# Layer 2 of a two-layer trunk: the transposes of a head's probabilities moved one weight block later

## The chip, the cores and the metric

One core of one Trainium2 chip runs the whole kernel. The metric is the device time of one execution in microseconds (us). Before the change it is 1230.51 us, the median of 3 runs (1229.99 to 1230.73).

## The reference

The input is a sequence of 256 tokens of width 2048. Layer 1 is a Mamba-2 layer, layer 2 a sparse latent attention layer with 32 heads of 128. The part that the change touches is the attention of layer 2, once the queries, the latent keys and values and the selection of keys are there:

```python
logits = jnp.einsum('bthc,btkc->bthk', ql, kv_sel).astype(jnp.float32) * attn_scale
valid = sel <= tpos[None, :, None]
logits = jnp.where(valid[:, :, None, :], logits, -jnp.inf)
pr = jax.nn.softmax(logits, -1).astype(kv_sel.dtype)
return jnp.einsum('bthk,btkc->bthc', pr, kv_sel)
...
o = jnp.einsum('bthc,hcv->bthv', o_lat, w_uv).reshape(b, L, DSA_WIDTH)
return (o * jax.nn.silu(gate)) @ w_out
```

The kernel computes it per head with keys and values expanded, and with a mask (`mb`) in place of the gathered rows. All matrix products of weights are in float32, split into a high and a low part.

## The kernel before

**Stream of weight blocks.** All weights go through one stream of units (class `Stream`, lines 62 to 167). A unit is one block of 128 x 1024 weights. For each unit SyncE loads `raw` (L94), ScalarE rounds it to `hi` (L110), VectorE computes `lo = raw - hi` (L139), and TensorE then multiplies with both. There are 4 buffers each of `raw`, `hi` and `lo`. `run` works through the units by position: at position i it first writes out the conversions up to unit i + 3, then the matmuls of unit i, then one step of every generator that is active (older ones first), and a generator that starts at i is added last. Every engine takes its instructions in just this order, and nothing reorders them later. When `lo` of a unit is written, the load of the unit 4 further on is issued.

**Heads stage.** Units are laid out per pair of heads p: one block for keys and values (`pair_a`, called A here), one for queries (`pair_b`, B), then one or two gate blocks of two units each (ga, gb: first and second half of a gate, `stream_w`). So the layout repeats every 10 blocks: A B ga gb A B ga gb ga gb. Counted from the first A of the stage as block 0, block 40 is the A of pair 8. Each A and each B has 24 matmuls; each half of a gate has 8 matmuls of 512 columns (L328) and 8 of 256 columns (L325).

**A head's steps** (`head_steps`). One step is taken behind each block. Counted from the step of the logits:

- step 0: logits `lg` on TensorE (L937 to L940)
- step 1: mask, scale and row minimum on VectorE, from PSUM into the tile `lgs` (L948)
- step 2: exponentials on ScalarE (L953), in place
- step 3: reciprocal and scaling on VectorE (L956, L958), in place
- step 5: three transposes of `lgs` on TensorE into the PSUM tile `pt` (L964)
- step 6: copies of `pt` on ScalarE (L968, L969) and the low part on VectorE (L970)
- step 8: output `o` (po) on TensorE (L974 to L977)
- step 9 to 11: product with the gate on VectorE (L980), then rounding (L987, L989)

Heads 4k to 4k+3 start (step 0) in blocks 10k+4, 10k+6, 10k+8 and 10k+10. For the group of heads 12 to 15 (blocks 34 to 40) and what follows, the steps that use TensorE or the tile `lgs` fall like this in the kernel before:

| block | kind | TensorE behind the block, in order | L948 into `lgs` |
|---|---|---|---|
| 39 | gb | transposes of head 12 | head 14, then in the buffer of head 12 |
| 40 | A | logits of 15 | |
| 41 | B | transposes of 13 | head 15, then in the buffer of head 13 |
| 42 | ga | output of 12 | |
| 43 | gb | transposes of 14 | |
| 44 | A | output of 13, logits of 16 | |
| 45 | B | transposes of 15 | head 16, then in the buffer of head 14 |
| 46 | ga | output of 14, logits of 17 | |
| 47 | gb | | head 17, then in the buffer of head 15 |
| 48 | ga | output of 15, logits of 18 | |
| 49 | gb | transposes of 16 | head 18, then in the buffer of head 16 |

**Buffers.** `lgs` has 2 buffers, so head h + 2 takes the one of head h and may write it only when the transposes of head h have read it. Logits and outputs share 2 PSUM buffers (`y_tile`) in the order in which they are issued: the logits of 16 take the buffer that the output of 12 had (free when L980 of head 12 has read it, block 43), the output of 14 takes that of the output of 13 (L980 of head 13, block 45), the logits of 18 take that of the logits of 17 (L948 of head 17, block 47). `pt` has 2 buffers. Gate, key and value sums share 3 buffers (`acc_tile`).

**Evacuation** of keys, values and queries (`evac_steps`): high part on ScalarE (L926), low part on VectorE (L927), a plain copy on ScalarE (L928), and for values L915, L916, L917. The two engines wait for each other in it. Of a gate, ScalarE copies one half of the sum (L333), VectorE adds the other (L336), ScalarE takes a tanh (L726), VectorE multiplies (L728).

Of the kernel before, what the change touches and what calls it, by code (L numbers as in the profile page):

```python
# [171 lines left out]
def trunk_kernel(ctx: ExitStack, tc: tile.TileContext, x, xt, w1, wdt, dtp, prm, wo1,  # L172
# [20 lines left out]
    def y_tile(name):  # L193
        return p_y.tile([P, 512], F32, tag="y", name=name)

    def m_tile(name):
        return p_m.tile([P, 512], F32, tag="m", name=name)
# [734 lines left out]
    def head_steps(h):  # L932
        p, k = divmod(h, 2)
        (qh, ql, q1), (kh, kl, k1) = ([a[:, k, :] for a in PR[p][nm]] for nm in "qk")
        vh, vl, v2 = (a[:, k * P:(k + 1) * P] for a in PR[p]["v"])
        pl = y_tile(f"lg{h}")
        nc.tensor.matmul(pl[:, 0:128], q1, k1, start=True, stop=True)  # L937
        nc.tensor.matmul(pl[:, 128:384], qh, kh, start=True, stop=False)
        nc.tensor.matmul(pl[:, 128:384], qh, kl, start=False, stop=False)
        nc.tensor.matmul(pl[:, 128:384], ql, kh, start=False, stop=True)  # L940
        yield
        lg = d2.tile([P, 384], F32, tag="lg", name=f"lgs{h}")
        mx = d2.tile([P, 2], F32, tag="mx", name=f"mx{h}")
        sm = d2.tile([P, 2], F32, tag="sm", name=f"sm{h}")
        rn = d2.tile([P, 2], F32, tag="rn", name=f"rn{h}")
        parts = ((0, 0, 128), (1, 128, 384))
        for j, a, b in parts:
            v.tensor_tensor_reduce(out=lg[:, a:b], in0=pl[:, a:b], in1=mb[:, a:b],  # L948
                                   scale=-ATT_SCALE, scalar=3.0e38, op0=ALU.add, op1=ALU.min,
                                   accum_out=mx[:, j:j + 1])  # L950
        yield
        for j, a, b in parts:
            nc.scalar.activation(lg[:, a:b], lg[:, a:b], AF.Exp, scale=-1.0,  # L953
                                 bias=mx[:, j:j + 1], accum_out=sm[:, j:j + 1])
        yield
        v.reciprocal(rn, sm)  # L956
        for j, a, b in parts:
            v.tensor_scalar(lg[:, a:b], lg[:, a:b], rn[:, j:j + 1], 0.5,  # L958
                            op0=ALU.mult, op1=ALU.mult)
        yield  # L960
        yield
        pt = m_tile(f"pt{h}")
        for a in (0, 128, 256):
            nc.tensor.transpose(pt[:, a:a + 128], lg[:, a:a + 128], ident)  # L964
        yield
        ph, pl = (d2.tile([P, T], F32R, tag=f"prT{j}", name=f"prT{h}_{j}") for j in range(2))
        p2 = d2.tile([P, P], F32, tag="prT2", name=f"prT{h}_2")
        nc.scalar.activation(ph, pt[:, 0:T], AF.Copy)  # L968
        nc.scalar.activation(p2, pt[:, T:384], AF.Copy)  # L969
        v.tensor_sub(pl, pt[:, 0:T], ph.bitcast(F32))  # L970
        yield
        yield
        po = y_tile(f"o{h}")
        nc.tensor.matmul(po[:, 0:T], vh, ph, start=True, stop=False)  # L974
        nc.tensor.matmul(po[:, 0:T], vh, pl, start=False, stop=False)
        nc.tensor.matmul(po[:, 0:T], vl, ph, start=False, stop=False)
        nc.tensor.matmul(po[:, P:T], v2, p2, start=False, stop=True)  # L977
        yield
        og = d2.tile([P, T], F32, tag="og", name=f"og{h}", bufs=3)
        v.tensor_mul(og, po[:, 0:T], GT.pop(h))  # L980
        if h == 0:
            OG.append(big.tile([P, KT, 2 * T], F32R, tag="A", name="og0"))
        if h == 16:
            OG.append(big.tile([P, KT, 2 * T], F32R, tag="C", name="og1"))
        dst = OG[h // 16][:, h % 16, :]
        yield
        nc.scalar.activation(dst[:, 0:T], og, AF.Copy)  # L987
        yield
        v.tensor_sub(dst[:, T:2 * T], og, dst[:, 0:T].bitcast(F32))  # L989
        yield  # L990
# [3 lines left out]
    for p in range(NH2 // 2):  # L994
        src = wab[2 * p]
        i = st.add(wab[2 * p], 1024, pair_a(p), MOVING)
        st.side(i, (evac_steps, p, ("k", "v")))
        i = st.add(wab[2 * p + 1], 1024, pair_b(p), MOVING)
        st.side(i, (evac_steps, p, ("q",)))
        st.side(i + 3, (head_steps, 2 * p))  # L1000
        st.side(i + 5, (head_steps, 2 * p + 1))
        n = (left * (p + 1)) // 16 - (left * p) // 16
        for _ in range(n):
            add_gate(next(gates))
# [342 lines left out]
```

## Time and profile before

| | |
|---|---|
| median of 3 runs | 1230.51 us |
| the profiled execution, its own time | 1230.21 us |
| span of the profiled execution, first to last instruction | 1228.5 us |
| heads stage (block 0 to the first block of the output projection) | about 770 to 1039.6 us of the span |
| 10 blocks of the heads stage | 33.7 us |

The span is 1.7 us shorter than the execution's own time; what lies around it is not in the trace. The page of the profile gives busy times by engine, the chain of work that ended last, and groups of instructions; the trace behind it gives single instructions with their start, their duration, the idle time of the engine before them and what ended it. Matmuls are pipelined: one starts before the one before it has ended, so the distance of starts is what a matmul costs TensorE, and not its duration.

### The profile page before, as it was taken

The numbers are of one execution on the slowest core, as the hardware profiler recorded it, in microseconds if no ns is written. First come the engines' busy times: TensorE is split into PE (matmuls) and PEld (weight loads), VectorE is DVE, ScalarE is ACT, GpSimd is POOL, SyncE is SP. The second block draws the span as 40 slices with busy tenths as digits, with TensorE's granted clock in tenths as the row PEclk, the third lists the DMA queues.
The fourth block names the chain that finished last, engine by engine and source line by source line (L and its number), as shares of the span: only waits on it lengthen the run. The fifth ranks groups of instructions, "written<-read, shape, count | busy, mean of one in ns | idle before, by whom it ended". The sixth has DMA issues, their size and how long they took to land.

```text
span 1228.5 us, 19506 instructions
## 1 busy us (share of the span) xinstructions
PE 1222.3 (99%) x7195; PEld 1063.6 (87%) x7195; DVE 935.7 (76%) x1757; ACT 701.6 (57%) x1274; POOL 65.6 (5%) x102
## 2 busy tenths in 40 slices
PE   9999999999999999999999999999999999999998
PEld 7888888888888888788888898999999999888886
DVE  6978788988898889757557778877777777667457
ACT  5666566666666666544336655566766666433341
POOL 0001011001100110110000000000000000000000
PEclk9999999999999999999999999999999999999999
DMA  8765666566666665677666564554444445875552
GB/s 290 215 201 179 207 185 213 171 209 188 203 183 207 187 205 182 190 226 229 200 192 200 196 209 146 168 170 164 161 154 149 161 155 188 311 232 184 200 194 98
DMA packets 65790, 236.55 MB, mean 193 GB/s; under 512 B 8072, under 2 KB 8208, under 8 KB 65312
## 3 DMA queue, kind: packets, MB, share of 16 engines
q1 hardware_dynamic: 60784, 215.29, 54.4%
q0 software_dynamic: 4912, 20.02, 5.2%
q8 instruction: 57, 0.93, 0.3%
q14 instruction: 37, 0.30, 0.1%
HBM read 231.00 MB, written 4.28 MB: 192 GB/s over the span
## 4 chain that ended last, share of the span: by engine, by line
PE 97%; DVE 2%; DMA 1%; issue 0%; ACT 0%; SPq 0%; DVEq 0%
PE acc L328 24%; PE acc L325 12%; PE g L328 10%; PE o L556 9%; PE o L557 9%; PE o L558 9%; PE g L325 5%; PE y L453 2%; PE q L902 1%; PE q L901 1%; PE q L903 1%; PE pt L964 1%; DVE lo L139 1%; PE pxs L433 1%; PE k L879 1%; PE k L880 1%
## 5 line engine op out<-in xcount | busy, mean ns | idle before, releaser
L139 DVE TENSOR_TENSOR lo<-raw,hi 128x1024 fp32r<-128x1024 f32 (+1 forms) x404 | 488.8, 1213 | 236.6 <-ACT hi L110 236.1
L110 ACT ACTIVATE hi<-raw 128x1024 fp32r<-128x1024 f32 (+2 forms) x405 | 421.6, 1048 | 207.6 <-PE o L558 156.1
L328 PE MATMUL acc<-xT,hi 128*128 128x512 f32 x1280 | 314.6, 394 | 0.9 <-ACT hi L110 0.9
L328 PEld LDWEIGHTS acc<-xT,hi 128*128 128x128 f32 x1280 | 232.8, 188 | 46.7 <-ACT hi L110 1.3
L325 PEld LDWEIGHTS acc<-xT,lo 128*128 128x128 f32 x1280 | 159.3, 188 | 6.5 <-DVE lo L139 0.2
L325 PE MATMUL acc<-xT,lo 128*128 128x256 f32 x1280 | 162.0, 278 | 0.0
L328 PE MATMUL g<-x1T,hi 128*128 128x512 f32 x512 | 127.4, 395 | 0.0
L328 PEld LDWEIGHTS g<-x1T,hi 128*128 128x128 f32 x512 | 92.5, 188 | 17.5
L556 PE MATMUL o<-hi,yg 128*128 128x512 f32 x256 | 100.4, 392 | 0.0
L558 PE MATMUL o<-hi,yg 128*128 128x512 f32 x256 | 99.7, 390 | 0.0
L557 PE MATMUL o<-lo,yg 128*128 128x512 f32 x256 | 99.7, 389 | 0.0
L556 PE MATMUL o<-hi,og 128*128 128x512 f32 (+1 forms) x256 | 99.6, 389 | 0.0
L558 PE MATMUL o<-hi,og 128*128 128x512 f32 (+1 forms) x256 | 98.9, 386 | 0.0
L557 PE MATMUL o<-lo,og 128*128 128x512 f32 (+1 forms) x256 | 98.9, 386 | 0.0
L355 DVE SCALAR_TENSOR_TENSOR ca<-cr,par,ca 128x255 f32<-128x255 f32 x144 | 69.2, 480 | 3.4
L325 PE MATMUL g<-x1T,lo 128*128 128x256 f32 x512 | 69.4, 280 | 0.0
L325 PEld LDWEIGHTS g<-x1T,lo 128*128 128x128 f32 x512 | 65.8, 188 | 2.9
L358 ACT ACTIVATE cr<-ca 128x256 f32<-128x256 f32 x48 | 20.1, 418 | 79.0 <-DVE ca L355 79.0
L556 PEld LDWEIGHTS o<-hi,yg 128*128 128x128 f32 x256 | 48.1, 188 | 10.2 <-issue 0.2
L558 PEld LDWEIGHTS o<-hi,yg 128*128 128x128 f32 x256 | 48.1, 188 | 10.1
L558 PEld LDWEIGHTS o<-hi,og 128*128 128x128 f32 x256 | 48.1, 188 | 9.9
L557 PEld LDWEIGHTS o<-lo,yg 128*128 128x128 f32 x256 | 48.1, 188 | 9.7
(274 smaller groups left out, 1781.0 us busy)
## 6 DMA issues: line engine op xcount, KB each, us to landing
raw<-in_w_dram SPq DMA_DIRECT2D x159, 512.0 KB, 4.2
raw<-in_wo_dram SPq DMA_DIRECT2D x128, 512.0 KB, 3.6
raw<-in_wg_dram SPq DMA_DIRECT2D x64, 512.0 KB, 3.2
raw<-in_wab_dram SPq DMA_DIRECT2D x32, 512.0 KB, 3.2
abc<-acs_d POOLq DMA_DIRECT2D x32, 256.0 KB, 4.1
raw<-in_wcq_dram SPq DMA_DIRECT2D x8, 512.0 KB, 4.3
raw<-in_wkv_dram SPq DMA_DIRECT2D x8, 336.0 KB, 3.0
rx<-in_x_dram POOLq DMA_DIRECT2D x2, 1024.0 KB, 11.2
```

The costliest lines, as they stand in the source:

```text
L110: self.nc.scalar.activation(h[:, cs], r[:, cs], AF.Copy)
L139: eng.tensor_sub(*self.halfway.pop(i))
L325: nc.tensor.matmul(ps[:, 0:T], lw, xs[:, kt, 0:T], start=False, stop=last, skip_group_check=True)
L328: nc.tensor.matmul(ps, h[:, w], xs[:, kt, :], start=(kt == 0), stop=last, skip_group_check=True)
L355: v.scalar_tensor_tensor(acc[:, d:], rw[:, :T - d], w(k), acc[:, d:], op0=ALU.mult, op1=ALU.add)
L358: nc.scalar.activation(rw, acc, AF.Tanh)
L433: nc.tensor.transpose(pm[:, o:o + P], G[g][("x", 2 * half + c)][:, s * P:(s + 1) * P], ident)
L453: nc.tensor.matmul(py[ks, c * T + s * P:(c + 1) * T], xsT[:, s, c, ks], ms[c][k][:, ws], start=(c == 0 and s == 0), stop=(s == 1), skip_gr ...
L556: nc.tensor.matmul(ps, ah, hs, start=(kk == 2 * first), stop=False)
L557: nc.tensor.matmul(ps, ah, ls, start=False, stop=False)
L558: nc.tensor.matmul(ps, al, hs, start=False, stop=(kk == 31))
L879: nc.tensor.matmul(ps, h[:, o:o + P], ckvT[:, ct, 0:T], start=(ct == 0), stop=False)
```

## The change

The transposes of a head's probabilities (L964) move from step 5 to step 6. They are now issued directly ahead of the copies of the same head, behind the matmuls of the block and behind whatever older heads issue there. In the table above, those of head 12 move from block 39 to block 40, ahead of the logits of 15; of 13 from 41 to 42, behind the output of 12; of 14 from 43 to 44 and of 15 from 45 to 46, between an output and logits. L948 of head h + 2 stays where it is. The copies, the outputs and all later steps of a head stay where they are. No tile, buffer count or instruction is added or removed.

```diff
                             op0=ALU.mult, op1=ALU.mult)
         yield
         yield
+        yield
+
         pt = m_tile(f"pt{h}")
         for a in (0, 128, 256):
             nc.tensor.transpose(pt[:, a:a + 128], lg[:, a:a + 128], ident)
-        yield
         ph, pl = (d2.tile([P, T], F32R, tag=f"prT{j}", name=f"prT{h}_{j}") for j in range(2))
```

## Rows read from the trace of the kernel before

**Rows 1.** The profile's page: busy time by engine, the TensorE clock in 40 slices (9 is 90% or more), and the chain that ended last by engine.
```profile
PE 1222.3 (99%) x7195; PEld 1063.6 (87%) x7195; DVE 935.7 (76%) x1757; ACT 701.6 (57%) x1274; POOL 65.6 (5%) x102
...
PEclk9999999999999999999999999999999999999999
...
PE 97%; DVE 2%; DMA 1%; issue 0%; ACT 0%; SPq 0%; DVEq 0%
```

**Rows 2.** Busy time of each engine in stretches of 10 blocks (blocks 40 to 49 and 50 to 59): the length in us, then PE, PEld, DVE, ACT and POOL busy with their instructions, the granted clock as a share of full speed, the DMA share and GB/s.
```profile
904.54:938.25 33.71, 33.71 (x247) 31.59 (x246) 25.58 (x62) 22.65 (x57) 0.00 (x0) 1.00 0.46 158
938.25:972.15 33.90, 33.90 (x247) 31.70 (x246) 25.22 (x61) 22.53 (x57) 0.00 (x0) 1.00 0.45 153
```

**Rows 3.** The instructions that use the tile `lgs`: what their engine waited for, in us in total and how often.
```profile
  PE pt L964: 4.2, 8
```

**Rows 4.** VectorE in order of time, blocks 39 to 42: start, duration, operation, and in brackets the idle time before it and what ended it. L948 is that of head 14.
```profile
904.82 0.29 DVE L948 CUSTOM_DVE_ANT_0 lgs<-lg,mb 128x128 f32<-128x128 f32 x1 [0.54 <-PE pt L964]
...
905.86 1.22 DVE L139 TENSOR_TENSOR lo<-raw,hi 128x1024 fp32r<-128x1024 f32 x1 [0.39 <-ACT hi L110]
...
907.67 0.41 DVE L336 TENSOR_TENSOR gate<-g,gate 128x256 f32<-128x256 f32 x1
908.00 0.68 DVE L927 TENSOR_TENSOR hk<-k,hk 128x512 fp32r<-128x512 f32 x1
...
910.63 1.22 DVE L139 TENSOR_TENSOR lo<-raw,hi 128x1024 fp32r<-128x1024 f32 x1 [0.52 <-ACT hi L110]
...
913.31 0.42 DVE L927 TENSOR_TENSOR hq<-q,hq 128x256 fp32r<-128x256 f32 x1
915.13 1.23 DVE L139 TENSOR_TENSOR lo<-raw,hi 128x1024 fp32r<-128x1024 f32 x1 [1.40 <-ACT hi L110]
```

**Rows 5.** ScalarE in order of time, in the same stretch.
```profile
908.72 0.38 ACT L928 ACTIVATE hk<-k 128x256 f32<-128x256 f32 x1 [0.79 <-DVE hk L927]
...
909.52 1.07 ACT L110 ACTIVATE hi<-raw 128x1024 fp32r<-128x1024 f32 x1
...
913.77 0.39 ACT L928 ACTIVATE hq<-q 128x256 f32<-128x256 f32 x1 [2.39 <-DVE hq L927]
914.05 1.05 ACT L110 ACTIVATE hi<-raw 128x1024 fp32r<-128x1024 f32 x1
```

**Rows 6.** TensorE in order of time: the transposes of head 12, the logits of head 15, the first matmul of block 41 (a B) and the transposes of head 13 behind its 24 matmuls.
```profile
904.29 0.49 PE L964 MATMUL pt<-ident,lgs 128*128 128x128 f32 x3
...
907.41 0.38 PE L937 MATMUL lg<-hk,hq 128*128 128x128 f32 x2
...
907.99 0.28 PE L901 MATMUL q<-cqT,hi 128*128 128x256 f32 x1
...
910.79 0.49 PE L964 MATMUL pt<-ident,lgs 128*128 128x128 f32 x3
```

**Rows 7.** VectorE: the products with the gate of heads 12 and 13, the low part of unit 50 (block 47) and the last instruction of head 17's L948 in blocks 43 to 47.
```profile
918.53 0.42 DVE L980 TENSOR_TENSOR og<-o,sC 128x256 f32<-128x256 f32 x1
...
925.42 0.42 DVE L980 TENSOR_TENSOR og<-o,sC 128x256 f32<-128x256 f32 x1
...
930.68 1.22 DVE L139 TENSOR_TENSOR lo<-raw,hi 128x1024 fp32r<-128x1024 f32 x1 [0.67 <-ACT hi L110]
...
933.70 0.08 DVE L948 DVE_READ_ACCUMULATOR2_ANT mx<- 128x1 f32 x1
```

**Rows 8.** TensorE's weight loads that come first in the logits of 16 (block 44), the output of 14 (block 46) and the logits of 18 (block 48).
```profile
920.84 0.30 PEld L937 LDWEIGHTS lg<-hk,hq 128*128 128x128 f32 x2
...
927.36 0.19 PEld L974 LDWEIGHTS o<-prT,hv 128*128 128x128 f32 x1
...
934.57 0.30 PEld L937 LDWEIGHTS lg<-hk,hq 128*128 128x128 f32 x2
```

**Rows 9.** The same place 10 blocks later (block 57 and 58): the last weight load of the output of 19, the last instruction of head 21's L948 on VectorE and the first weight load of the logits of 22.
```profile
968.06 0.31 PEld L977 LDWEIGHTS o<-prT,hv 128*128 128x128 f32 x2
...
968.30 0.08 DVE L948 DVE_READ_ACCUMULATOR2_ANT mx<- 128x1 f32 x1
...
968.44 0.30 PEld L937 LDWEIGHTS lg<-hk,hq 128*128 128x128 f32 x2
```

**Rows 10.** The same place in the first group (blocks 17 and 18): head 5's L948 and the logits of 6.
```profile
832.26 0.08 DVE L948 DVE_READ_ACCUMULATOR2_ANT mx<- 128x1 f32 x1
...
833.43 0.30 PEld L937 LDWEIGHTS lg<-hk,hq 128*128 128x128 f32 x2
```

**Rows 11.** The chain that ended last in order of time: start and length of its pieces, with the number of instructions. Three transposes, the 8 matmuls of 512 columns behind them, 16 such matmuls behind matmuls of the stream, and the two matmuls that open the logits (L937: 128 columns in plain float32, as the transposes are; the stream's and most others are in the rounded type).
```profile
910.95 0.33 PE pt L964 x3
911.28 1.85 PE g L328 x8
...
929.69 3.65 PE g L328 x16
...
934.84 0.22 PE lg L937 x2
```

**Rows 12.** VectorE early in the output projection (units 87 and 88).
```profile
1055.40 1.23 DVE L139 TENSOR_TENSOR lo<-raw,hi 128x1024 fp32r<-128x1024 f32 x1 [3.00 <-ACT hi L110]
...
1059.73 1.22 DVE L139 TENSOR_TENSOR lo<-raw,hi 128x1024 fp32r<-128x1024 f32 x1 [2.78 <-ACT hi L110]
```

**Rows 13.** The page's DMA issues: loads of gate weights, count, size and median us to landing.
```profile
raw<-in_wg_dram SPq DMA_DIRECT2D x64, 512.0 KB, 3.2
```

## The prediction

> **What bounds the kernel now.** I read the page first: TensorE is busy 99% of the span, the chain that ended last runs 97% over it, and its granted clock is full in all slices [rows 1]. Then I read the heads stage in stretches of 10 blocks: TensorE is busy for every microsecond of 33.71, VectorE for 25.58 and ScalarE for 22.65 [rows 2]. So a change in this stage is worth what it does to TensorE: instructions that it spares, or waits that it puts in front of it. VectorE's and ScalarE's own idle time costs nothing until it reaches a buffer that TensorE wants. Then I asked who waits for the transposes: VectorE, in L948, for 4.2 us in 8 places, and nobody else of weight [rows 3]. That is one wait in each group of four heads, and it is the wait that this change moves.
>
> **Part 1, the transposes for themselves.** A turning is three transposes, 0.33 us on the chain; the 8 wide matmuls behind it take 1.85 us, where 16 such matmuls behind others take 3.65, or 1.83 for 8 [rows 11]. So a turning between two stretches of the stream costs 0.33 + 0.02 = 0.35 us. Between an output, which ends in plain float32, and logits, which begin so, I take three times what one of the two L937 takes, 3 x 0.11 = 0.33 [rows 11], with no second change of type. Saved: 0.02 us for each of 32 heads, 0.6 us in all. Not seen in the trace: transposes directly behind an output. Its bounds are no saving at all and the whole 0.35 us (32 x 0.35 = 11 us), but the three transposes are still issued and 0.33 of the 0.35 are theirs, so I take 0.02.
>
> **Part 2, the copies.** ScalarE's copies now follow their transposes in the same step, and wait for the end of the block. For head 12 that is some 1.6 us later than before; behind them in ScalarE's queue are the exponentials of head 14, which wait for L948 anyway (part 3). For heads 13 to 15 the copies come into ScalarE's queue after the transposes, once the delay of part 3 is counted. The output stands two blocks behind the copies as before. I cost this part at nothing; its cover is those two blocks, and without it the output would wait.
>
> **Part 3, L948 waits for a whole block.** L948 of head h + 2 needs the buffer of head h. For the first two heads of each group of four, heads h and h + 2 start 4 blocks apart, so L948 stands in step 5 of head h: until now directly behind the transposes, and after the change one block *ahead* of them. VectorE works in order, so it stands still until TensorE is through the next block and the transposes behind it. Nothing deadlocks: block 40 needs nothing that stands behind L948 of head 14.
>
> How much later: the transposes of head 12 start at 904.29, and L948 of head 14 at 904.82, 0.53 later [rows 4, 6]. After the change block 40 starts where those transposes did, and its 24 matmuls take 2.80 us (a block B with as many: 907.99 to 910.79 [rows 6]). So L948 starts 2.80 us later, at about 907.62. Queued behind it are the low part of unit 43, the low part of head 12's copies, the gate sum (L336), then keys and values of pair 8.
>
> What of it comes back: the low part of unit 43 had waited 0.39 us for ScalarE [rows 4]; ScalarE has it ready by then, so the lag falls to 2.80 - 0.39 = 2.41 us. From there on nothing comes back, and this is the point of the whole argument. The idle times of VectorE behind it (0.52 and 1.40 us in rows 4, 0.67 in rows 7) all end by ScalarE's rounding, and ScalarE's idle times ahead of those roundings (0.79 and 2.39 us [rows 5]) all end by VectorE's L927. The two hand work to and fro in evacuation: L927 at 913.31, L928 at 913.77, rounding at 914.05, low part at 915.13 [rows 4, 5]. So both keep a lag of 2.41 us, idle or not, up to L948 of head 17. The second L948 in this position (head 15, which now waits for head 13's transposes, behind block 42) adds none: by the same lag the L927 directly behind it (913.31 [rows 4]) comes at 915.7, and those transposes are read from about 914.7 on (907.09 + 0.33 + the logits' 0.58 + 2.80 for block 41 + 2.8 for block 42 + an output's 0.58 is 914.2, and 0.53 more).
>
> When TensorE meets it: it wants shared PSUM buffers. Handing over costs 0.06 us: where L948 of head 21 ended at 968.38, the weights of the logits were loaded at 968.44 and not, as usual, 0.2 us earlier [rows 9]. Margins before, less 0.06:
> - gate sum of block 39, wanted by block 42 at about 910.7: L336 ends 908.08 [rows 4] + 2.41 = 910.5. No wait, by 0.2 us.
> - logits of 16: L980 ends 918.95, the load starts 920.84 [rows 7, 8]: 1.83. Wait 0.58.
> - output of 14: 925.84 to 927.36: 1.46 [rows 7, 8]. TensorE is 0.95 late here.
> - logits of 18: L948 of head 17 ends 933.78, the load starts 934.57: 0.73 [rows 7, 8]. TensorE is 2.41 - 0.73 = 1.68 us late here.
>
> These don't add up, since the lag is carried by VectorE and ScalarE and each wait pays a part of it: the last and largest counts, 1.68 us for a group. Behind it comes the next L948 that waits for transposes, now behind block 50, and VectorE is there before TensorE: the lag begins anew and isn't summed.
>
> By groups: of 8, the last has its L948 in the output projection, where there are no evacuations and VectorE idles 3.00 and 2.78 us at a time [rows 12]; its cover is that idleness, and I cost it at nothing (if it went, at most another 1.7 us). Of the other seven, the first had a margin of 833.43 - 832.34 - 0.06 = 1.03 [rows 10], so 1.38 us; in the fifth the margin is already gone (blocks 50 to 59 take 33.90 us [rows 2, 9]), so 2.41; five take 1.68. Sum: 1.38 + 5 x 1.68 + 2.41 = 12.2 us. Since TensorE waits for VectorE in these groups, the savings of part 1 in them are not additional; only the last group's count, 0.1 us.
>
> **SyncE's loads** are issued when a low part is done, so some come 2.4 us later. A load lands in 3.2 us [rows 13] and its unit is rounded four units further on, over 10 us later; nothing waits. POOL has no work in these stretches [rows 2].
>
> **Sum.** 1230.21 + 12.2 - 0.1 = 1242.3 us against the profiled execution's own time; that one is 0.30 under the median of the runs, so 1242.6 for a median. I say 1242.5, +1.0%.
>
> **The rivals.**
> - *On the other side: no wait reaches TensorE.* VectorE and ScalarE are idle a quarter of the time and more [rows 2] and could win the lag back before block 48. It decides at 2.41 - 0.73: if they regain 1.7 us of the 2.41, TensorE notices nothing and only part 1 is left, 1230.5 - 0.6 = 1229.9, no difference that can be measured. It also covers the case that the buffer isn't awaited as I read it. Against it: the idle times named above are waits of the two for each other. The Trainium skill, in "Perfetto Trace Analysis", section "Identifying the Most-Contended Engine", has occupancy name the engine to work on. By that rule TensorE's own work would decide and this rival would be the forecast; rows 9, where a late L948 holds up a TensorE that is busy 100%, speak against it. 9%. Faster by over 0.2% would need 2.5 us, 0.08 for each turning, four times what the rows give: 3%.
> - *Half of it.* ScalarE comes to the wait with work done ahead, and 1 us more is regained than the 0.39. Then the groups cost 0.4 + 5 x 0.7 + 1.4 = 5.3 us: 1235.8. For it: exponentials and copies of one group change their order in time. 10%.
> - *All of it and more.* The two engines regain nothing, not even the 0.39, and TensorE's new waits hold back sums that they in turn need (ScalarE waits for gate sums of TensorE in each group). With the whole 2.80 us for each of seven groups: 1230.5 + 19.6 = 1250. 6%.
> - *The clock.* TensorE would have three short waits in each group. No row of before shows its clock below full, the level of 2.4 GHz [rows 1, 2], with a wait as short as that of rows 9. The Trainium skill, in "TensorE: Matmul & The Clock Gate", section "A second HAM failure mode: psum-queue depth-cycling", tells of short idle times between groups of matmuls that made the clock swing between its two levels. One stretch of 10 blocks at half the clock would cost up to 33.7 us more: 1276. 2%.
>
> **How the numbers follow.** The forecast has 70%, with a range of its own of 1239 to 1246: 0.5 us of error in the lag or in a margin makes 7 x 0.5 = 3.5 us. The rivals have 9, 3, 10, 6 and 2%. To hold 8 in 10 the range takes in the half case below and the full case above: 1234 to 1250. A measurement of this kernel tells about 0.2%, or 2.5 us, from no change. Faster by more: 3%. Within it: 9%. Slower: 88%.
>
> **What would show it.** In the trace after: L948 of the third head of each group with an idle time of some 3 us ended by the transposes, where it had 0.54 [rows 4]; the copies and L927 behind it some 2.4 us later against TensorE; stretches of 10 blocks of about 35.4 us with TensorE idle in front of logits and outputs, ended by VectorE's L980 and L948. Part 1 would show as turnings of 0.33 us and wide matmuls of 1.83 behind logits. I am wrong if L948 doesn't idle, if it does and the stretches stay at 33.7, or if TensorE's waits end by anything else than VectorE.

## The result, and the profile after

The changed kernel takes 1242.04 us (median of 5 runs, 1241.33 to 1242.54), against 1230.51 before: a ratio of 1.0094 (95% interval 1.0082 to 1.0105). The forecast was 1242.5 with a range of 1234 to 1250. The profiled execution took 1241.33 us, with a span of 1239.5, 11.0 more than before. All medians here and below are of executions at the full clock: one execution of the kernel e8, below, took 1765.66 us at a granted clock of 0.647 and is not counted in its median.

The page of the profile says little: VectorE and ScalarE are as busy as before in us, TensorE stands at 99% still, and its clock is full.

```profile
PE 1227.0 (99%) x7195; PEld 1065.1 (86%) x7195; DVE 935.0 (75%) x1757; ACT 700.4 (57%) x1274; POOL 65.6 (5%) x102
...
PEclk9999999999999999999999999999999999999999
```

The same stretches as in [rows 2], blocks 40 to 49 and 50 to 59, tell where the time went. They have grown from 33.71 and 33.90 to 35.31 and 36.19 us, and TensorE is no longer busy for all of it: 34.48 and 34.43. In the first stretch the idle 0.83 us are half of the 1.60 us more; the other 0.77 stand in the busy time of the same matmuls, whose ends are modelled. So what a wait costs TensorE is read from starts, further down and in the part on the prediction.

```profile
908.44:943.75 35.31, 34.48 (x246) 31.92 (x245) 25.53 (x64) 22.43 (x56) 0.00 (x0) 1.00 0.45 150
943.75:979.94 36.19, 34.43 (x246) 31.88 (x245) 25.57 (x64) 22.43 (x56) 0.00 (x0) 1.00 0.44 146
```

Taken from the first matmul of each group's first block to the next, for the seven groups from block 10 to the output projection (a lateness was forecast for each):

| group from block | 10 | 20 | 30 | 40 | 50 | 60 | 70 | sum |
|---|---|---|---|---|---|---|---|---|
| before, us | 33.69 | 33.71 | 33.71 | 33.71 | 33.90 | 33.71 | 33.71 | 236.1 |
| after, us | 34.98 | 35.30 | 35.29 | 35.31 | 36.19 | 35.31 | 35.29 | 247.7 |
| growth, us | 1.29 | 1.59 | 1.58 | 1.60 | 2.29 | 1.60 | 1.58 | 11.5 |
| growth forecast, us | 1.38 | 1.68 | 1.68 | 1.68 | 2.41 | 1.68 | 1.68 | 12.2 |

The seven groups have grown by 11.5 us, which is the whole of the span's 11.0 and 0.5 more: block 10 begins 0.56 us earlier than before (802.87 against 803.43, in part because the first transposes now stand behind it), and from the output projection on both take the same time (188.9 us to the end).

Who waits for the transposes, the view of [rows 3] for the kernel after, first what the engine in question waited for:

```profile
  PE pt L966: 23.2, 9
...
  DVE lgs L948: 23.2, 9
  ACT prT L969: 14.6, 9
  PEld lg L937: 3.2, 7
```

4.2 us of VectorE's waiting have become 23.2; ScalarE's copies (L969 now) wait for 14.6 us, which they did not before, both 9 times. The last row is a weight load of logits that stands directly behind transposes; what it really waits for is shown with the three places of TensorE below.

VectorE in blocks 39 to 47, for [rows 4, 7]. L948 of head 14 has stood idle for 2.58 us; the low part behind it has no idle time now, where it had 0.39.

```profile
911.74 0.29 DVE L948 CUSTOM_DVE_ANT_0 lgs<-lg,mb 128x128 f32<-128x128 f32 x1 [2.58 <-PE pt L966]
...
912.30 1.22 DVE L139 TENSOR_TENSOR lo<-raw,hi 128x1024 fp32r<-128x1024 f32 x1
...
914.11 0.41 DVE L336 TENSOR_TENSOR gate<-g,gate 128x256 f32<-128x256 f32 x1
...
917.07 1.23 DVE L139 TENSOR_TENSOR lo<-raw,hi 128x1024 fp32r<-128x1024 f32 x1 [0.52 <-ACT hi L110]
...
919.76 0.42 DVE L927 TENSOR_TENSOR hq<-q,hq 128x256 fp32r<-128x256 f32 x1
921.58 1.22 DVE L139 TENSOR_TENSOR lo<-raw,hi 128x1024 fp32r<-128x1024 f32 x1 [1.40 <-ACT hi L110]
...
924.97 0.42 DVE L981 TENSOR_TENSOR og<-o,sC 128x256 f32<-128x256 f32 x1
...
931.86 0.42 DVE L981 TENSOR_TENSOR og<-o,sC 128x256 f32<-128x256 f32 x1
...
937.12 1.23 DVE L139 TENSOR_TENSOR lo<-raw,hi 128x1024 fp32r<-128x1024 f32 x1 [0.67 <-ACT hi L110]
...
940.14 0.08 DVE L948 DVE_READ_ACCUMULATOR2_ANT mx<- 128x1 f32 x1
```

Read the idle times against [rows 4, 7]: 0.52, 1.40 and 0.67 us, each the same to the hundredth. They win nothing back. From L948 of head 14 to the end of head 17's it is 940.22 - 911.74 = 28.48 us, against 933.78 - 904.82 - 0.39 = 28.57 before without that one idle time.

TensorE in the three places of [rows 8]. First the logits of 16, whose matmul names VectorE as what ended its wait (L956 is the instruction directly behind L981 in VectorE's order), then the weight loads of all three:

```profile
925.54 0.46 PE L937 MATMUL lg<-hk,hq 128*128 128x128 f32 x2 [0.30 <-DVE rn L956]
```

```profile
925.51 0.30 PEld L937 LDWEIGHTS lg<-hk,hq 128*128 128x128 f32 x2 [0.51 <-PE pt L966]
...
932.39 0.19 PEld L975 LDWEIGHTS o<-prT,hv 128*128 128x128 f32 x1 [0.64 <-issue]
...
940.28 0.30 PEld L937 LDWEIGHTS lg<-hk,hq 128*128 128x128 f32 x2 [0.24 <-DVE mx L948]
```

All three wait. Each load starts 0.06 to 0.12 us behind the end of what frees its buffer by the order of buffers: L981 ends at 925.39 and the load starts at 925.51; L981 ends at 932.28, the load 932.39; L948 ends at 940.22, the load 940.28. These are the three waits that were worked out, in the three places. The first row names L966, the transposes ahead of the load, as what ended its wait, but their matmuls end at 925.23, 0.28 us ahead of it; by the buffers it is L981. The second names nothing ("issue"); its matmul, in the part on the prediction, names L981.

### The profile page after: what moved, and what is told of

Same layout as the page of the kernel before. It is cut to its first block, busy times and chain, and to the rows that moved or that the text cites. A ratio compares the mean times of both kernels' runs of the same rounds, so it can differ in the third digit from the quotient of the medians.

```text
span 1239.5 us, 19505 instructions
## 1 busy us (share of the span) xinstructions
PE 1227.0 (99%) x7195; PEld 1065.1 (86%) x7195; DVE 935.0 (75%) x1757; ACT 700.4 (57%) x1274; POOL 65.6 (5%) x102
## 4 chain that ended last, share of the span: by engine, by line
PE 84%; DVE 8%; ACT 4%; issue 2%; DMA 1%; SPq 0%; DVEq 0%; ACTq 0%
PE acc L328 22%; PE acc L325 11%; PE o L556 9%; PE o L558 9%; PE o L557 9%; PE g L328 6%; DVE lo L139 4%; PE g L325 3%; ACT hi L110 3%; PE y L453 2%; DVE lgs L948 1%; DVE hk L927 1%; PE pxs L433 1%; DMA raw<-in_w_dram 1%; PE qp L697 1%
```

## The experiments

Three theories were on record before the runs. A: L948's wait for the buffer of `lgs` is the whole cost. B: ScalarE's copies, which now stand in the step of their transposes, wait for the end of the block too, and this was only hidden behind A. C: the transposes cost TensorE more where they stand now.

**A third buffer for `lgs`.** Room for it comes from a constant of layer 1 that moves into layer 1's own pool.

```diff
-    sel = cpool.tile([P, 2, P], F32, tag="sel", name="sel")
...
+    sel = sp1.tile([P, 2, P], F32, tag="sel", name="sel")
...
-        lg = d2.tile([P, 384], F32, tag="lg", name=f"lgs{h}")
+        lg = d2.tile([P, 384], F32, tag="lg", name=f"lgs{h}", bufs=3)
```

> The changed kernel with a third buffer for the tile lgs (and the constant tile sel of layer 1 in layer 1's own pool, to make room). Theory A, the wait of L948 for the transposes is the whole cost: 1229.9 us, stretches of 10 blocks of 33.7. Theory B, ScalarE's copies behind the transposes wait for the end of the block as well and were only hidden behind A: head 12's copies come 1.6 us later, the key evacuation behind them 1.58 later; against the margins of 1.03, 0.73 and 0 of the groups that is 0.55 + 5 x 0.85 + 1.58 = 6.4, so 1236.8 us. Theory C, the transposes cost more where they now stand on TensorE (12 us over 32 turnings, 0.37 each): 1242.

Measured: 1236.16 us, ratio to before 1.0053 (1.0041 to 1.0066); groups of 34.55 us. So A takes half of the loss with it and no more; B's number was 1236.8. The trace shows B's chain. ScalarE, then VectorE, in blocks 40 and 41:

```profile
909.55 0.38 ACT L969 ACTIVATE prT<-pt 128x256 fp32r<-128x256 f32 x1 [1.49 <-PE pt L966]
909.83 0.27 ACT L970 ACTIVATE prT<-pt 128x128 f32<-128x128 f32 x1
...
910.87 0.59 ACT L926 ACTIVATE hk<-k 128x512 fp32r<-128x512 f32 x1
```

```profile
906.85 0.28 DVE L948 CUSTOM_DVE_ANT_0 lgs<-lg,mb 128x128 f32<-128x128 f32 x1
...
910.13 0.42 DVE L971 TENSOR_TENSOR prT<-pt,prT 128x256 fp32r<-128x256 f32 x1 [1.12 <-PE lg L940]
...
911.49 0.69 DVE L927 TENSOR_TENSOR hk<-k,hk 128x512 fp32r<-128x512 f32 x1 [0.27 <-ACT hk L926]
```

L948 waits no longer, but the copies do, and VectorE then waits twice for ScalarE: for the low part of the copies and for the rounding of the keys, which stands behind the exponentials behind the copies. The row of the first wait names a matmul of the logits, L940, as what ended it. But L971 starts at 910.13, when ScalarE's second copy ends (L970, 909.83 + 0.27 = 910.10), and over the whole run the view of the tile `pt` names that copy in six of nine such places:

```profile
  ACT prT L970: 6.7, 6
  PE lg L940: 3.4, 3
```

The control, the kernel before with the same third buffer:

> The kernel before with the same third buffer and the same move of sel: a control. By all theories 1230.3 us (VectorE's 0.54 us waits in L948 go, and with them at most the 0.2 us that the fifth group loses); a difference from before would belong to the buffer itself.

Measured: 1230.45 us, ratio 1.0002 (0.9993 to 1.0011), groups of 33.71. The buffer by itself does nothing.

**The copies one step later as well**, with three buffers, first for the first head of each group (`later` is `h % 4 in (0,)`, e6), then for the first and third (e7, shown):

```diff
+        later = h % 4 in (0, 2)
+        if later:
+            yield
         ph, pl = (d2.tile([P, T], F32R, tag=f"prT{j}", name=f"prT{h}_{j}") for j in range(2))
...
         yield
-        yield
+        if not later:
+            yield
         po = y_tile(f"o{h}")
```

> As e1_three_buffers, and the copies of the first head of each group one step later, so that ScalarE no longer waits for the end of the block A there. Theory B: what is left is the same wait of the third head's copies behind the other A of a group, with a lag of 0.95 us; 5 x 0.22 + 0.95, less a little: 1232.4 us. Theory A: 1229.9. Theory C: 1242.

> As e1_three_buffers, and the copies of the first and the third head of each group one step later. Theory B: no wait of 0.73 us or more is left, only a lag of 0.34 in the fifth group, and part 1's saving of 0.02 for each turning shows: 1230.2 us. Theory A: 1229.9. Theory C: 1242.

Measured: 1233.31 us, ratio 1.0025 (1.0015 to 1.0035), with groups of 34.11; and 1231.47 us, ratio 1.0009 (1.0000 to 1.0018), with groups of 33.75. The loss goes step by step with the two waits of ScalarE, as B has it. The first is 0.9 us over its number. Its groups have grown by about 0.40 us in six cases, where 0.22 had been reckoned for five and nothing for the first, and by 0.21 in the fifth, where 0.95 had been reckoned; together 2.67 us against 2.05. What is left of the 0.9 isn't explained. The next experiment shows that term by itself.

**The transposes later for some heads only**, two buffers (e3, shown; in e4 `late` is `h % 4 == 0`, in e5 `h % 4 == 1`):

```diff
         yield
         yield
+        late = h % 4 >= 2
+        if late:
+            yield
         pt = m_tile(f"pt{h}")
...
-        yield
+        if not late:
+            yield
```

> The kernel before, with the later transposes only for the third and fourth head of each group, whose buffer of lgs nobody wants a block earlier. Theory A: 1230.2 us. Theory B: the third head's copies wait for the end of an A, a lag of 0.95 us against margins of 1.03, 0.73 and 0: 5 x 0.22 + 0.95 = 2.1, so 1232.4 us. Theory C, by the place of the transposes: half of the loss, 1236.

> The kernel before, with the later transposes only for the first head of each group. Theories A and B: the whole loss, since this wait is the longest and the second adds none: a lag of 2.41 us, 1242.4 us. Theory C: a quarter of the loss, 1233.5.

> The kernel before, with the later transposes only for the second head of each group. Theory A: the transposes of head 13 are read from 914.68 on, L948 of head 15 was at 912.76, a lag of 1.92 us; less the margins 0.89 + 5 x 1.19 + 1.92 = 8.8, so 1239.3 us. If only the first head's wait did harm: 1230.4. Theory C: a quarter of the loss, 1233.5.

Measured: for the third and fourth heads (e3) 1233.41 us, ratio 1.0021 (1.0012 to 1.0030), groups of 34.10 to 34.13, 1.0 over B's number. For the first head (e4) 1241.93 us, 1.0094 (1.0080 to 1.0107), groups of 35.29, the whole loss from 8 of 32 turnings. For the second (e5) 1239.8 us, 1.0075 (1.0061 to 1.0088), groups of 34.9. Its group has +1.21 us, where 1.92 - 0.73 = 1.19 was expected. C, which goes by the number of turnings, had 1236, 1233.5 and 1233.5, and is out. e5 is also the plainest case of A: ScalarE's copies wait for transposes only once in the whole run there, so L948's wait does its harm alone. L948 of head 15 in e5, which does wait here:

```profile
919.16 0.29 DVE L948 CUSTOM_DVE_ANT_0 lgs<-lg,mb 128x128 f32<-128x128 f32 x1 [1.82 <-PE pt L967]
```

In e3 L948 waits for transposes no more (0.3 us once in the heads stage), and B's wait of the third head stands alone. ScalarE, then VectorE, in block 24:

```profile
854.44 0.39 ACT L972 ACTIVATE prT<-pt 128x256 fp32r<-128x256 f32 x1 [1.78 <-PE pt L967]
```

```profile
855.02 0.42 DVE L974 TENSOR_TENSOR prT<-pt,prT 128x256 fp32r<-128x256 f32 x1 [1.02 <-ACT prT L973]
```

VectorE's low part starts when the *second* copy (L973) has ended, 0.58 us after the first has started. VectorE's lag is 1.1 us, where 0.95 was reckoned: the rounding of keys behind it (L927) starts 855.69 - 837.80 = 17.89 us after the group's first matmul, before the change 853.89 - 837.11 = 16.78. Less the margin of 0.73 that is 0.4, the growth of the groups. The fifth group grows by 0.23 only. There VectorE is late in block 54 already before the change, by an idle time that the other groups don't have, and the new wait hides behind it: L974 comes 17.23 us after the group's first matmul, where the same instruction came 17.01 after it.

```profile
954.12 1.23 DVE L139 TENSOR_TENSOR lo<-raw,hi 128x1024 fp32r<-128x1024 f32 x1 [0.80 <-ACT hi L110]
...
955.26 0.41 DVE L970 TENSOR_TENSOR prT<-pt,prT 128x256 fp32r<-128x256 f32 x1
```

These are rows of the kernel before. From this idle time on VectorE is 0.9 us later than in the fourth group (17.01 against 16.11 for L970), more than the margin of 0.73, so that the fifth group has none left.

**L948's wait without ScalarE's**: two buffers, and the later copies of e7 (e8).

> The changed kernel with its two buffers of lgs, and the copies of the first and the third head of each group one step later, so that ScalarE waits for the end of no block A; L948 still does. If L948's wait alone makes the changed kernel's loss and the copies' wait only stood in its shadow: 1241 to 1242.5 us, stretches of 35.1 to 35.3. If the two waits add up, the copies' part (5 to 6 us by e1_three_buffers) goes: 1236. If the copies' wait is the cause and L948's is not: 1231.5, as e7_copies_both.

Measured: 1247.91 us, ratio 1.0143 (1.0126 to 1.0160): more than the changed kernel, which none of the three cases had. The same kernel once more, for its trace (e9):

> The kernel of e8_two_buffers_copies_both once more, for a profile at the full clock; its time was 1247.9 us, 6 more than every theory had. Expected: 1247.9 us, stretches of 10 blocks of about 36.1, and the trace shows what is added to L948's wait. By theory A with the late copies in the path: L948's lag of 2.41 us, and the copies' low part (L970), which now stands a block later between L948 and TensorE's next need, added to it. By a rival, the output waits for its own late copies: TensorE's idle times then end by L970 and not by L980 or L948.

Measured: 1246.2 us in one run, groups of 35.9 us. TensorE's weight loads wait, and by this view the first of them for the late copies' low part (L974):

```profile
PEld o L980 <- DVE prT L974: 6.1, 7, 0.9
...
PEld o L979 <- issue: 3.2, 7, 1.2
PEld lg L937 <- DVE mx L948: 3.0, 7, 0.4
```

L948's wait is there undiminished (2.59 us for head 14), so it needs no help from the copies; but the late copies now come behind it in VectorE's order and into the path of the output. Both things that the expectation had as rivals happen: waits that end by L974, and waits that end by L948. The trace also tells how the 0.6 us more for each group (35.87 against 35.30) come about. VectorE's late L974 makes the output of 12 wait, the transposes of head 13 stand behind that output, and L948 of head 15 now waits for them, which it doesn't in the changed kernel:

```profile
919.98 0.42 DVE L974 TENSOR_TENSOR prT<-pt,prT 128x256 fp32r<-128x256 f32 x1
...
920.45 0.39 PE L980 MATMUL o<-prT,hv 128*128 128x256 f32 x1 [0.71 <-DVE prT L974]
...
921.54 0.29 DVE L948 CUSTOM_DVE_ANT_0 lgs<-lg,mb 128x128 f32<-128x128 f32 x1 [0.48 <-PE pt L966]
```

From L948 of head 14 to the end of head 17's it is 942.57 - 913.51 = 29.06 us, where the changed kernel has 28.48: 0.58 more, and 0.48 of it is this second wait. So e8 doesn't take ScalarE's part away cleanly, and doesn't tell what L948's wait costs without it; e5 does, for the second head.

No run beats the kernel before. e2 can't be told from it, and e7, which has the transposes where the change puts them and none of the waits of L948 and TensorE, is 0.09% above it, with an interval that begins at no difference.

## Why the prediction was right

- **Part 3, the mechanism.** Right in its steps, with one size off: the wait of L948 (2.58 us idle), the 0.39 us that come back and next to nothing more, the lag carried unshortened through the work that the two engines hand to and fro, TensorE stopped in three places by the buffers named, the last one counting. The loop was reckoned at 33.71 + 1.68 = 35.39 us and is 35.30. The rest of 0.09 is the chain itself, 28.48 against 28.57. The size that was off is the second of the three waits, as e7 shows, which issues the same matmuls in the same order without these waits. Logits of 16, output of 14 and logits of 18, first in the changed kernel (its block 40 starts at 908.43), then in e7 (904.48):

```profile
932.43 0.36 PE L975 MATMUL o<-prT,hv 128*128 128x256 f32 x1 [0.47 <-DVE og L981]
...
940.28 0.49 PE L937 MATMUL lg<-hk,hq 128*128 128x128 f32 x2
```

```profile
921.14 0.39 PE L937 MATMUL lg<-hk,hq 128*128 128x128 f32 x2
...
927.33 0.28 PE L979 MATMUL o<-prT,hv 128*128 128x256 f32 x1
...
934.90 0.39 PE L937 MATMUL lg<-hk,hq 128*128 128x128 f32 x2
```

  With 925.54 for the first place, shown above, TensorE is late there by 0.45, 1.15 and 1.43 us, and by 1.56 at the end of the group (35.31 against 33.75); the forecast was 0.58, 0.95 and 1.68. The margin of 1.46 us at the output of 14 had the transposes of head 15 ahead of it, in block 45. The change puts them behind that output, so TensorE arrives 0.33 us earlier and the margin is 1.13; the lag of 2.32 (2.41 - 0.09) less 1.13 is 1.19. It made no difference to the sum, because the third wait counts, and no transposes change sides there.
- **The second L948 adds none.** Right: e4 alone has the whole loss. Yet by itself it costs some 9 us (e5); it stands in the first one's shadow, which the text said.
- **Groups and sum.** First, fifth and the other groups as forecast, each 0.1 us less; 11.5 against 12.2 us. The last group costs nothing, as taken: the output projection is as long as before.
- **Part 2 was costed for the wrong reason.** "I cost this part at nothing; its cover is those two blocks, and without it the output would wait." The cover was not those blocks but L948's own longer wait. Once that is gone (e1), the copies' wait costs 5.7 us against the control (1236.16 - 1230.45). It does so not by an output that waits for its copies, but by the rounding of keys and the low part that stand behind the copies on the two engines and come late. The half sentence that head 14's exponentials wait for L948 anyway was the right cover; its price without it should have been worked out.
- **Part 1 saved nothing.** "A turning between two stretches of the stream costs 0.33 + 0.02." The trace of e7, where no wait hides it, has turnings of 0.33 us, and the wide matmuls behind a B, with no transposes between, still take 1.85:

```profile
907.43 0.33 PE pt L966 x3
907.76 0.22 PE lg L937 x2
...
911.15 1.85 PE g L328 x8
...
920.98 0.33 PE pt L966 x3
921.31 0.22 PE lg L937 x2
```

  So the 0.02 go with the block ahead and not with the turning. Groups of 33.75 (e7) against 33.71 (e2) show no saving of 0.02 x 4, rather 0.04 us more. It made no difference to the forecast, since in seven groups the saving was not counted.
- **The rivals.** That no wait reaches TensorE fell with the idle times above. The Trainium skill, in "Perfetto Trace Analysis", section "Identifying the Most-Contended Engine", names the engine to work on by occupancy. The trace agrees on the engine, TensorE with 99%, but its matmuls are as many after the change (7195 in both) and the time is not the same. The half case and the full case fell: the 0.39 us came back, and 0.09 beside them. The clock stayed at its full level of 2.4 GHz, 1.00 in both stretches, through three waits in each group.

## What to carry to other kernels

Where a step is moved behind other work, look first for who waits for its *inputs* to be read: a buffer that is overwritten two heads later can put a wait a whole block deep into an engine that had time to spare. Such an engine's idle time is no reserve if it is spent waiting for a partner that waits for it; the lag then runs on until a buffer that the busy engine wants, and the smallest margin there, not the share of idle time, gives the price. Take the margins in the order that the change makes: work that it puts behind such a place no longer counts for its margin. And when one wait hides another, price the hidden one too: taking the first away with a third buffer gave back half.

## What was not expected of the hardware

Not expected was that the VectorE instruction L974 of e3, which needs only the first of ScalarE's two copies out of the same PSUM tile, started when the second had ended as well (0.58 us behind the start of the first, its idle time of 1.02 us ended by the second). In e1 it is 0.58 us as well (909.55 to 910.13). The view finds by semaphores what ended a wait, which speaks for a wait that is written in the program; whether the chip alone would let the instruction start earlier, the runs don't tell. And three transposes in plain float32 take 0.33 us on the chain wherever they stand: between a B and a gate block of the stream [rows 11] and between an output and logits (920.98 in e7, above) alike.
